# Group norm of the short convolution: products and copies four blocks ahead of the subtractions, and the gate norm's first sums of squares behind the gate's silu

## The chip, the cores and the metric

The kernel runs on one core of one Trainium2 chip. The metric is the device time of one execution in microseconds. The kernel before takes 1411.71 us (median of 3 runs, 1411.12 to 1412.81).

Engine names as the profile has them: PE is TensorE (matmuls; PEld is its weight load), DVE is VectorE, ACT is ScalarE, POOL is GpSimd, SP is the queue that issues most DMAs.

## The reference, cut to what matters

One layer over 1024 tokens of width 1024: a mixer, then a mixture of experts with 32 experts. The change touches the mixer, between its last projections and its output matmuls:

```python
def grouped_rmsnorm(x, g, n_groups):
    shp = x.shape
    xf = x.astype(jnp.float32).reshape(*shp[:-1], n_groups, shp[-1] // n_groups)
    y = xf * lax.rsqrt(jnp.mean(xf * xf, axis=-1, keepdims=True) + EPS)
    return (y.reshape(shp) * g.astype(jnp.float32)).astype(x.dtype)
...
    ssd_out = grouped_rmsnorm(y * jax.nn.silu(z), ssd_norm, SSD_GROUPS)
    sc = sc_b * causal_depthwise_conv(sc_c * sc_v, sc_conv_w)
    sc_out = grouped_rmsnorm(sc, sc_norm, SC_GROUPS)
    return jnp.concatenate([ssd_out, sc_out], axis=-1) @ w_out
```

`SSD_GROUPS` is 2 (groups of 512 columns), `SC_GROUPS` is 16 (groups of 64).

## The kernel before, in words

The tokens are worked through in two halves of 512 (`h` = 0 and 1). Each half runs 61 blocks of matmuls on PE, in a fixed order: 1 block `dt`, 12 `xbc`, 24 of the short convolution (`c`, `v`, `b`), 8 `z` (the gate), then `s` 0 to 3, `d` 0 to 3, `s` 4 to 7, `d` 4 to 7. The `s` and `d` blocks together are the output matmul: an `s` block multiplies the normed short convolution (`SCT`), a `d` block the normed gated part (`SST`), and both sum in one PSUM bank. The experts follow after the second half.

Everything is float32, split in two float32r parts: a matmul of two such numbers is three matmuls (high by high, high by low, low by high), so a block is 8 x 3 = 24 matmuls. The split of a 128x1024 piece of weights (`split_w`) is a copy on ACT (L80, `copy_a`) into the high half of a buffer `W` (four of them, `W[b % 4]`), and a subtraction on DVE (L86, `tt`) into the low half. In block n's turn the weights of block n + 3 are split.

The order of the work of each engine is the order in which the program issues it; each engine works in that order and waits by semaphores. The loop over blocks (`for n in range(NB)`) does in each turn: what follows from the block before (`post`), the block's matmuls, the load and split of weights ahead, and then the steps which a table has put on that turn (`at(n, f, ...)`, `todo`). The change is in that table. Steps around it, with b0 = 1 for the first half and 62 for the second, so that b0 + 41 is the sixth of the eight `z` blocks, b0 + 44 is the block `s` 0:

- `z_post` (L561): when the last of four `z` blocks is done, ACT takes the silu of its four PSUM banks into four temporaries, and DVE multiplies the four into `Y`. The last four silus stand in the turn of `s` 0, behind the weight copy of the turn before.
- `sc_norm_out` (lines 465 to 476): for each of 8 blocks j, DVE multiplies the short convolution by its weight and by its group's reciprocal root (L83, `SC<-SC,pc,P`), ACT copies the product into the high half of `SCT` (L80, `TB<-SC` in the first half, `TA<-SC` in the second), and DVE subtracts for the low half (L86). It is called for pairs of blocks: two products, two copies, two subtractions.
- `y_stats` (L568): sums of squares of `Y` on ACT, four for each group of 512 columns; the first group's need only the first four `z` blocks.
- `y_norm`: a square root on ACT (a table load, L90), a reciprocal on DVE (L91), and eight scalings of `Y` on DVE (L576), the first group's four ahead of the second's.
- `y_out` (L255): transposes of the scaled `Y` on PE, for columns 0 and 1 behind `s` 1, for 2 to 4 behind `s` 2, for 5 to 7 behind `s` 3.

PSUM has four banks `acc`. The four `z` banks are open until the last `z` block; the bank of `s` 0 is the first of these, free when the first silu has read it.

Of the kernel before, what the change touches and what calls it, by code (L numbers as in the profile page):

```python
# [36 lines left out]
def layer(ctx: ExitStack, tc: tile.TileContext, x, norm_mix, w_mix, ssd_conv_w, ssd_conv_b, dt_bias,  # L37
# [15 lines left out]
    def region(tag, shape, dt=F32):  # L53
        return rg.tile(shape, dt, name=tag, tag=tag)
# [24 lines left out]
    def copy_a(o, i, scale=1.0):  # L79
        act.activation(o, i, AF.Copy, scale=scale)  # L80

    def stt(o, a, s, b, op0, op1):
        dve.scalar_tensor_tensor(o, a, s, b, op0=op0, op1=op1)  # L83

    def tt(o, a, b, op):
        dve.tensor_tensor(o, a, b, op=op)  # L86
# [16 lines left out]
    def PC(i):  # L103
        return pc[:, i:i + 1]
# [143 lines left out]
    def halves(o, k, pt, scale):  # L248
        copy_a(o[:, 0, k], pt, scale=scale)
        stt(o[:, 1, k], pt, scale, o[:, 0, k].bitcast(F32), OP.mult, OP.subtract)  # L250
# [12 lines left out]
    def at(n, f, *a):  # L263
        todo.setdefault(n, []).append((f, a))
# [203 lines left out]
    def sc_norm_out(h, js):  # L468
        if js[0] == 0:
            SCT[h] = region(TA_IN[1 - h], [P, 2, KD, TB], FR)  # L470
        for j in js:
            o = SC[h][:, j]
            stt(o, o, PC(100 + j), RB[h][:, j], OP.mult, OP.mult)
            copy_a(SCT[h][:, 0, j], o)
        for j in js:
            tt(SCT[h][:, 1, j], SC[h][:, j], SCT[h][:, 0, j].bitcast(F32), OP.subtract)

# [409 lines left out]
    for h in range(2):  # L887
        b0 = h * HB + 1
        at(b0 + 1, dt_turn, h)
        at(b0 + 3, cum_mm, h)  # L890
        at(b0 + 4, cum_out, h)
        at(b0 + 37, sc_root, h)
        for u in range(8):
            at(b0 + max(11, 10 + 3 * u), ssd_seg_load, h, u)
            at(b0 + (12 + 3 * u if u else 13), ssd_decay, h, u)
            at(b0 + 13 + 3 * u, ssd_t, h, u)
            at(b0 + 14 + 3 * u, ssd_e, h, u)
            at(b0 + 15 + 3 * u, ssd_m, h, u)
            at(b0 + 16 + 3 * u, ssd_post, h, u)
        at(b0 + 38, silu_ready)  # L900
        for j in range(0, 8, 2):
            at(b0 + 41 + j // 4, sc_norm_out, h, (j, j + 1))
        at(b0 + 42, y_stats, h, 0)
        at(b0 + 44, y_stats, h, 1)
        at(b0 + 44, y_norm, h)
        for n, ks in ((45, (0, 1)), (46, (2, 3, 4)), (47, (5, 6, 7))):
            at(b0 + n, y_out, h, ks)
        at(b0 + 43, o_room, h)
        for j in range(8):
            nd = b0 + 48 + j + (4 if j > 3 else 0)  # L910
            at(nd - 1, x_load, h, j)
        if h == 1:
            for q, n in enumerate((44, 44, 45, 46, 51, 47, 49, 55, 56, 57, 57, 58, 58)):
                at(b0 + n, load_m, q)
            at(b0 + 50, h_diag)
        if h == 0:
            at(b0 + 46, lambda: X.__setitem__(1, region("SC", [P, KD, TB])))
            for q in range(4):
                at(b0 + 46, load_xT, 1, q)
            for i in range(NT):  # L920
                at(b0 + 5 + i, prep_stats, 1, i)
            at(b0 + 9, prep_root, 1, 0, 4)
            at(b0 + 45, g2_load)
            at(b0 + 51, root_first)
            for k in range(KD):
                at(b0 + 53 + k // 4, x_root, k)
            at(b0 + 56, lambda: XT.__setitem__(1, region(TA_IN[1], [P, 2, KD, TB], FR)))
            for k in range(KD):
                at(b0 + 56 + k // 2, lambda k=k: halves(XT[1], k, X[1][:, k], PC(k)))
            at(b0 + 28, route_load)  # L930
            at(b0 + 32, route_const)
            at(b0 + 46, route_weights)
            e0 = b0 + HB + 2
            at(e0 + 1, h_root, 0)
            at(e0 + 2, h_rows, 0)
            at(e0 + 3, h_cols, 0)
            at(e0 + 4, route_choose, 0)
            at(e0 + 6, route_pos_mm, 0)
            at(e0 + 7, route_gates, 0)
            at(e0 + 7, route_pos, 0)  # L940
            for part in range(2):
                at(e0 + 10 + part, route_tab, 0, part)
                at(e0 + 10 + part, route_tab_out, 0, part)
# [4 lines left out]
    for n in range(NB):  # L948
        kind, h, j = blocks[n][:3]
# [417 lines left out]
```

## Time and profile before

| what | us |
|---|---|
| median of 3 runs (lowest to highest) | 1411.71 (1411.12 to 1412.81) |
| the profiled execution's own time | 1409.6 |
| its span, from the first to the last instruction | 1407.8 |
| PE busy in the span | 1355.8 |
| DVE busy | 1047.1 |
| ACT busy | 888.2 |
| mean granted TensorE clock, share of full speed | 0.982 |

The span is what the trace shows; 1.8 us lie around it. A busy share is an average over stages; here what counts are the places where PE, the busiest engine, stands still. In a timeline each row is one instruction, or several alike in a row: start, length, engine, line, operation, tiles, and in brackets how long the engine was idle before it and what released it.

### The profile page before, as it was taken

Reading aid. Unit: us, or ns where it says so; the run is one execution under the profiler, and the core shown is the slowest. Engines: PE = TensorE matmul, PEld = TensorE weight load, DVE = VectorE, ACT = ScalarE, POOL = GpSimd, SP = SyncE. Lnnn points to the kernel's source line nnn. Section 1 sums busy time; section 2 is a strip of 40 time slices with the busy share of each in tenths; the row PEclk is TensorE's granted clock in tenths of the full one; section 3 lists DMA queues with packets and bytes.
Section 4 is the critical chain, followed back from the end, with each engine's and each line's share of the span. In section 5 each row is a group of like instructions: output and inputs, shape, how many; then the busy total and the mean of one; then the engine's idle time right before and its main releaser. Section 6 shows DMA issues by size and latency. Waiting matters only on the chain. (4 is left out here: it accounts for less than half of the span.)

```text
span 1407.8 us, 17291 instructions
## 1 busy us (share of the span) xinstructions
PE 1355.8 (96%) x6354; PEld 1071.5 (76%) x6354; DVE 1047.1 (74%) x1390; ACT 888.2 (63%) x1322; POOL 135.9 (10%) x124
## 2 busy tenths in 40 slices
PE   7999999989999999999999799999999999999992
PEld 5888887878878878788788677777777777777771
DVE  5776667574567776665643589999999999999985
ACT  6665443353475644344643488888888888888884
POOL 0000101000000000000000102211212211111110
PEclk9999999999999999999999899999999999999996
DMA  7243322534353232324556789999999999997996
GB/s 303 91 148 136 95 83 82 150 135 151 113 157 136 90 120 84 111 90 117 213 193 228 253 305 367 359 380 345 356 366 369 361 359 377 390 374 278 375 365 254
DMA packets 73176, 325.93 MB, mean 232 GB/s; under 512 B 11079, under 2 KB 27863, under 8 KB 40576
## 3 DMA queue, kind: packets, MB, share of 16 engines
q1 hardware_dynamic: 60816, 294.89, 55.9%
q0 software_dynamic: 12272, 29.90, 8.1%
q8 instruction: 51, 0.84, 0.2%
q14 instruction: 37, 0.30, 0.1%
HBM read 312.31 MB, written 29.49 MB: 243 GB/s over the span
## 5 line engine op out<-in xcount | busy, mean ns | idle before, releaser
L86 DVE TENSOR_TENSOR W<-WR,W 128x1024 fp32r<-128x1024 f32 x160 | 194.5, 1221 | 90.8 <-ACT W L80 90.3
L80 ACT ACTIVATE W<-WR 128x1024 fp32r<-128x1024 f32 x160 | 167.8, 1053 | 70.6 <-PE acc L270 37.0
L1182 PE MATMUL acc<-W,TB 128*112 128x512 f32 x512 | 204.7, 400 | 0.0
L1184 PE MATMUL acc<-W,TB 128*112 128x512 f32 x512 | 202.8, 396 | 0.0
L1183 PE MATMUL acc<-W,TB 128*112 128x512 f32 x512 | 200.8, 392 | 0.1
L269 PE MATMUL acc<-TB,W 128*128 128x512 f32 x416 | 166.7, 401 | 4.7 <-ACT tk L561 4.7
L269 PE MATMUL acc<-TA,W 128*128 128x512 f32 x416 | 166.1, 399 | 2.1 <-ACT tk L561 2.1
L271 PE MATMUL acc<-TA,W 128*128 128x512 f32 x416 | 162.9, 392 | 0.5 <-DVE W L86 0.5
L271 PE MATMUL acc<-TB,W 128*128 128x512 f32 x416 | 163.0, 392 | 0.0
L270 PE MATMUL acc<-TB,W 128*128 128x512 f32 x416 | 162.9, 392 | 0.0
L270 PE MATMUL acc<-TA,W 128*128 128x512 f32 x416 | 162.7, 391 | 0.0
L86 DVE TENSOR_TENSOR W<-SC,W 128x1024 fp32r<-128x1024 f32 x96 | 114.3, 1219 | 14.7 <-ACT W L80 14.7
L86 DVE TENSOR_TENSOR W<-Y,W 128x1024 fp32r<-128x1024 f32 x92 | 109.5, 1218 | 10.7 <-ACT W L80 10.5
L1183 PEld LDWEIGHTS acc<-W,TB 128*112 128x112 f32 x512 | 90.0, 176 | 28.7 <-DVE W L86 0.5
L1184 PEld LDWEIGHTS acc<-W,TB 128*112 128x112 f32 x512 | 89.2, 174 | 29.6 <-DVE TB L86 0.2
L1182 PEld LDWEIGHTS acc<-W,TB 128*112 128x112 f32 x512 | 89.2, 174 | 27.1 <-ACT TB L80 0.2
L86 DVE TENSOR_TENSOR W<-P,W 128x1024 fp32r<-128x1024 f32 (+1 forms) x82 | 96.0, 1196 | 13.0 <-ACT W L80 13.0
L1193 PE MATMUL sd<-W,TB 128*112 128x512 f32 x256 | 103.9, 406 | 0.8 <-ACT TB L80 0.6
L80 ACT ACTIVATE W<-SC 128x1024 fp32r<-128x1024 f32 x96 | 98.2, 1059 | 6.7 <-PE sd L1195 2.9
L1195 PE MATMUL sd<-W,TB 128*112 128x512 f32 x256 | 101.9, 398 | 0.0
L1194 PE MATMUL sd<-W,TB 128*112 128x512 f32 x256 | 101.2, 395 | 0.0
L80 ACT ACTIVATE W<-Y 128x1024 fp32r<-128x1024 f32 x92 | 94.8, 1060 | 10.0 <-PE sd L1195 4.0
(322 smaller groups left out, 2463.0 us busy)
## 6 DMA issues: line engine op xcount, KB each, us to landing
WR<-in_w_mix_dram SPq DMA_DIRECT2D x60, 1024.0 KB, 4.9
SC<-in_w_down_dram SPq DMA_DIRECT2D x18, 1024.0 KB, 7.5
SC<-in_w_gate_dram SPq DMA_DIRECT2D x16, 1024.0 KB, 7.6
P<-in_w_up_dram SPq DMA_DIRECT2D x16, 1024.0 KB, 7.4
Y<-in_w_up_dram SPq DMA_DIRECT2D x16, 1024.0 KB, 7.7
Y<-in_w_gate_dram SPq DMA_DIRECT2D x15, 1024.0 KB, 7.5
TA<-in_w_down_dram SPq DMA_DIRECT2D x15, 1024.0 KB, 8.0
Y<-in_w_down_dram SPq DMA_DIRECT2D x15, 1024.0 KB, 7.3
```

The source lines that it names most:

```text
L80: act.activation(o, i, AF.Copy, scale=scale)
L86: dve.tensor_tensor(o, a, b, op=op)
L269: pe.matmul(o, w[:, 0, k], t[:, 0, k], start=start and k == 0, stop=False)
L270: pe.matmul(o, w[:, 0, k], t[:, 1, k], start=False, stop=False)
L271: pe.matmul(o, w[:, 1, k], t[:, 0, k], start=False, stop=stop and k == KD - 1)
L1182: pe.matmul(pt, a[:, 0, k], w[:, 0, q], start=k == 0, stop=False)
L1183: pe.matmul(pt, a[:, 0, k], w[:, 1, q], start=False, stop=False)
L1184: pe.matmul(pt, a[:, 1, k], w[:, 0, q], start=False, stop=k == KD - 1)
L1193: pe.matmul(pt, a[:, 0, k], w[:, 0, n], start=k == 0, stop=False)
L1194: pe.matmul(pt, a[:, 0, k], w[:, 1, n], start=False, stop=False)
L1195: pe.matmul(pt, a[:, 1, k], w[:, 0, n], start=False, stop=k == 3)
```

## The change

The subtractions get a function of their own, `sc_norm_rest`, and the table is changed. Before: two pairs of blocks each in turns b0 + 41 and b0 + 42, and `y_stats` of the first group at b0 + 42. Now products and copies of blocks 0 to 3 stand in turn b0 + 41 with the subtractions of 0 and 1; the rest in b0 + 42; and the first group's `y_stats` is moved to b0 + 44, straight ahead of the second's.

```diff
@@ -472,6 +472,8 @@
             o = SC[h][:, j]
             stt(o, o, PC(100 + j), RB[h][:, j], OP.mult, OP.mult)
             copy_a(SCT[h][:, 0, j], o)
+
+    def sc_norm_rest(h, js):
         for j in js:
             tt(SCT[h][:, 1, j], SC[h][:, j], SCT[h][:, 0, j].bitcast(F32), OP.subtract)
 
@@ -898,9 +900,13 @@
             at(b0 + 15 + 3 * u, ssd_m, h, u)
             at(b0 + 16 + 3 * u, ssd_post, h, u)
         at(b0 + 38, silu_ready)
-        for j in range(0, 8, 2):
-            at(b0 + 41 + j // 4, sc_norm_out, h, (j, j + 1))
-        at(b0 + 42, y_stats, h, 0)
+        at(b0 + 41, sc_norm_out, h, (0, 1, 2, 3))
+        at(b0 + 41, sc_norm_rest, h, (0, 1))
+        at(b0 + 42, sc_norm_out, h, (4, 5))
+        at(b0 + 42, sc_norm_rest, h, (2, 3))
+        at(b0 + 42, sc_norm_out, h, (6, 7))
+        at(b0 + 42, sc_norm_rest, h, (4, 5, 6, 7))
+        at(b0 + 44, y_stats, h, 0)
         at(b0 + 44, y_stats, h, 1)
         at(b0 + 44, y_norm, h)
```

The order of the instructions changes on ACT and DVE alone, at one place in each half; on PE, POOL and SP every row stands where it stood. The two places of the first half follow (the second half's read alike, with `TA` for `TB`). Lines from 475 on are two higher in the changed kernel, so L563 is the silu that was L561 and L570 the sum of squares that was L568.

ACT, first half, from the weight copy of turn b0 + 41 to the square root of the gate norm; `TB<-SC` is the copy of a product into `SCT`, `W_84` the buffer of the weights of `s` 2, `tk<-acc` the silu. Before:

```order
L80 ACTIVATE W_82<-WR 128x1024
L80 ACTIVATE TB<-SC 128x512 x4
L80 ACTIVATE W_83<-WR 128x1024
L80 ACTIVATE TB<-SC 128x512 x4
L568 ACTIVATE junk,ssz<-Y 128x512 x4
L80 ACTIVATE W_84<-WR 128x1024
L561 ACTIVATE tk<-acc,rsx 128x512 x4
L80 ACTIVATE W_81<-WR 128x1024
L568 ACTIVATE junk,ssz<-Y 128x512 x4
L90 ACT_TABLE_LOAD
L90 ACTIVATE rsz<-ssz,eps 128x8
```

and of the change:

```order
L80 ACTIVATE W_82<-WR 128x1024
L80 ACTIVATE TB<-SC 128x512 x4
L80 ACTIVATE W_83<-WR 128x1024
L80 ACTIVATE TB<-SC 128x512 x4
L80 ACTIVATE W_84<-WR 128x1024
L563 ACTIVATE tk<-acc,rsx 128x512 x4
L80 ACTIVATE W_81<-WR 128x1024
L570 ACTIVATE junk,ssz<-Y 128x512 x8
L90 ACT_TABLE_LOAD
L90 ACTIVATE rsz<-ssz,eps 128x8
```

The four sums of the first group no longer stand ahead of the silu; all eight stand between the weight copy behind it and the square root.

DVE, first half, the same stretch, from the subtraction for the weights of `s` 0 to the multiplication of the silus into `Y`; `SC<-SC,pc,P` is a product, `TB<-SC,TB` a subtraction of the short convolution. Before:

```order
L86 TENSOR_TENSOR W_82<-WR,W_82 128x1024
L83 SCALAR_TENSOR_TENSOR SC<-SC,pc,P_1904 128x512 x2
L86 TENSOR_TENSOR TB<-SC,TB 128x512 x2
L83 SCALAR_TENSOR_TENSOR SC<-SC,pc,P_1904 128x512 x2
L86 TENSOR_TENSOR TB<-SC,TB 128x512 x2
L86 TENSOR_TENSOR W_83<-WR,W_83 128x1024
L83 SCALAR_TENSOR_TENSOR SC<-SC,pc,P_1904 128x512 x2
L86 TENSOR_TENSOR TB<-SC,TB 128x512 x2
L83 SCALAR_TENSOR_TENSOR SC<-SC,pc,P_1904 128x512 x2
L86 TENSOR_TENSOR TB<-SC,TB 128x512 x2
L86 TENSOR_TENSOR W_84<-WR,W_84 128x1024
L86 TENSOR_TENSOR Y<-Y,tk 128x512 x4
```

and of the change:

```order
L86 TENSOR_TENSOR W_82<-WR,W_82 128x1024
L83 SCALAR_TENSOR_TENSOR SC<-SC,pc,P_1904 128x512 x4
L86 TENSOR_TENSOR TB<-SC,TB 128x512 x2
L86 TENSOR_TENSOR W_83<-WR,W_83 128x1024
L83 SCALAR_TENSOR_TENSOR SC<-SC,pc,P_1904 128x512 x2
L86 TENSOR_TENSOR TB<-SC,TB 128x512 x2
L83 SCALAR_TENSOR_TENSOR SC<-SC,pc,P_1904 128x512 x2
L86 TENSOR_TENSOR TB<-SC,TB 128x512 x4
L86 TENSOR_TENSOR W_84<-WR,W_84 128x1024
L86 TENSOR_TENSOR Y<-Y,tk 128x512 x4
```

Two subtractions have moved from ahead of the weights of `s` 1 (`W_83`) to behind them, and the last products stand ahead of four subtractions instead of two.

## Rows read from the trace of the kernel before

**Rows 1.** Page: busy us of each engine, share of the span, instructions
```profile
PE 1355.8 (96%) x6354; PEld 1071.5 (76%) x6354; DVE 1047.1 (74%) x1390; ACT 888.2 (63%) x1322; POOL 135.9 (10%) x124
```

**Rows 2.** Waits of PE: line, releaser, us in total, times, longest us
```profile
PE acc L269 <- ACT tk L561: 6.8, 2, 4.7
```

**Rows 3.** Timeline of PE, first half, around the block s 0 and the first transposes
```profile
292.91 0.39 PE L290 MATMUL acc<-W,TA 128*128 128x512 f32 x1
...
293.59 0.39 PE L290 MATMUL acc<-W,TA 128*128 128x512 f32 x1
298.71 0.79 PE L269 MATMUL acc<-TB,W 128*128 128x512 f32 x1 [4.73 <-ACT tk L561]
...
312.04 1.03 PE L255 MATMUL sd<-ident,Y 128*128 128x128 f32 x8
312.83 0.48 PE L269 MATMUL acc<-TB,W 128*128 128x512 f32 x1
```

**Rows 4.** Timeline of PE, second half, the same places
```profile
685.99 0.39 PE L290 MATMUL acc<-W,TB 128*128 128x512 f32 x1
688.45 0.50 PE L269 MATMUL acc<-TA,W 128*128 128x512 f32 x1 [2.07 <-ACT tk L561]
...
701.87 0.48 PE L269 MATMUL acc<-TA,W 128*128 128x512 f32 x1
```

**Rows 5.** Timeline of ACT, first half, from the last copies to the square root's table
```profile
292.97 1.29 ACT L80 ACTIVATE TB<-SC 128x512 fp32r<-128x512 f32 x2 [1.42 <-DVE SC L83]
294.17 0.61 ACT L568 ACTIVATE junk<-Y 128x512 bf16<-128x512 f32 x1
...
297.04 1.04 ACT L80 ACTIVATE W<-WR 128x1024 fp32r<-128x1024 f32 x1
297.99 2.41 ACT L561 ACTIVATE tk<-acc,rsx 128x512 f32<-128x512 f32 x4
300.27 1.07 ACT L80 ACTIVATE W<-WR 128x1024 fp32r<-128x1024 f32 x1
301.21 0.64 ACT L568 ACTIVATE junk<-Y 128x512 bf16<-128x512 f32 x1
...
304.23 1.28 ACT L90 ACT_TABLE_LOAD   x1
```

**Rows 6.** Timeline of DVE, first half, the norm of the short convolution and the scalings
```profile
282.56 1.41 DVE L83 SCALAR_TENSOR_TENSOR SC<-SC,pc,P 128x512 f32<-128x512 f32 x2
284.00 1.35 DVE L86 TENSOR_TENSOR TB<-SC,TB 128x512 fp32r<-128x512 f32 x2
285.27 1.41 DVE L83 SCALAR_TENSOR_TENSOR SC<-SC,pc,P 128x512 f32<-128x512 f32 x2
...
288.33 1.23 DVE L86 TENSOR_TENSOR W<-WR,W 128x1024 fp32r<-128x1024 f32 x1 [0.26 <-ACT W L80]
...
306.09 3.25 DVE L576 TENSOR_SCALAR Y<-Y,rsz 128x512 f32<-128x512 f32 x8
```

**Rows 7.** Timeline of ACT, second half, the square root's table
```profile
693.70 1.28 ACT L90 ACT_TABLE_LOAD   x1
```

**Rows 8.** Timeline of DVE, second half, the first products and the scalings
```profile
672.38 1.41 DVE L83 SCALAR_TENSOR_TENSOR SC<-SC,pc,P 128x512 f32<-128x512 f32 x2
...
695.56 3.26 DVE L576 TENSOR_SCALAR Y<-Y,rsz 128x512 f32<-128x512 f32 x8
```

**Rows 9.** Stretches: us, PE, PEld, DVE, ACT, POOL busy (count); then PEclk, DMA share, GB/s
```profile
24.00:28.00 4.00, 3.28 (x19) 2.60 (x19) 2.37 (x10) 1.73 (x3) 0.00 (x0) 1.00 0.89 302
...
298.00:303.50 5.50, 4.79 (x11) 3.80 (x12) 4.77 (x6) 5.41 (x13) 0.00 (x0) 0.50 0.00 0
...
688.40:693.00 4.60, 4.55 (x13) 3.61 (x14) 4.32 (x6) 4.50 (x11) 0.00 (x0) 0.63 0.66 274
```

**Rows 10.** Timeline of PE, an early short pause
```profile
24.90 1.33 PE L234 MATMUL sd<-tk,ones 128*128 128x128 f32 x8 [0.72 <-DVE tk L233]
```

**Rows 11.** Waits of the SP queue: the loads of the experts' weights (L871)
```profile
SPq L871 <- DVE W L86: 452.8, 159, 14.5
```

## The prediction

> **What bounds the kernel now.** I read the page first: PE is busy for 96% of the span [rows 1], so time can come only from its pauses, from a lower clock behind them, or from its work, which the change leaves alone. The waits of PE come second: its largest wait in total is that of the first matmul of `s` 0 (L269) for the gate's silu on ACT (L561), twice, 6.8 us, the longest 4.7 [rows 2]. So the change sits at PE's costliest wait. Third, the timelines around them.
>
> At full clock matmuls follow each other every 0.227 us (three steps from 292.91 to 293.59 [rows 3]). In the first half the last matmul of `z` starts at 293.59; the next could start at 293.82 and starts at 298.71 [rows 3]: 4.89 us lost. In the second half it could start at 686.22 and starts at 688.45 [rows 4]: 2.23 us lost. A second loss follows the pause. The granted clock from 298 to 303.5 is 0.50, which is the 1.2 GHz level, and 0.63 in the mean from 688.4 to 693 [rows 9]. From the start of `s` 0 to that of `s` 2 there are 48 matmuls (48 x 0.227 = 10.88 us) and eight transposes (312.04 to 312.83, 0.79 us), 11.67 us at full clock. They take 312.83 - 298.71 = 14.12 [rows 3] and 701.87 - 688.45 = 13.42 [rows 4]: the clock costs 2.45 and 1.75.
>
> What holds the silu? ACT ends its last copy of the short convolution at 294.26, then does four sums of squares (294.17 to 297.04) and the weight copy for `s` 2 (297.04), and only then the silu, at 297.99; the matmul follows 0.72 later [rows 3, 5]. PE was done with `z` at 293.98. So four sums that nobody needs yet stand ahead of the silu, and behind the copies, which wait for products on DVE.
>
> **The change, part by part.** No instruction is added or taken away.
>
> *Sums moved.* Without them ACT goes from the last copy to the weight copy 2.87 us earlier (297.04 - 294.17) [rows 5].
>
> *Products and copies ahead.* On DVE two products take 1.44 us to the next row's start (282.56 to 284.00), two subtractions 1.27, a weight subtraction 1.23 in all [rows 6]. New order from 282.56: four products end at 285.44, two subtractions at 286.71. Copy 3 ends on ACT at 286.1 (the fourth product's end 285.4 and half of a pair's 1.29 [rows 5]), the weight copy for `s` 1 at 287.1 (1.04 [rows 5]); DVE waits 0.4 for it, instead of 0.26 now, and subtracts until 288.3. Two products, two subtractions, two products end at 292.45, and the last copy, 0.65 long, ends at 293.1 instead of 294.26. The weight copy then starts at about 293.05, since these two overlap a little now too (294.17 against 294.26 [rows 5]). The four subtractions at the end take DVE to 295.0, as before; the last is needed by the 23rd matmul of `s` 0, 5 us into the block.
>
> *Start of `s` 0, first half.* Weight copy at 293.05, silu at 294.0 (0.95 later, as now), matmul at 294.72 instead of 298.71: **3.99 us earlier**, 0.9 behind an unbroken run. A pause of 0.72 early in the kernel left the clock at 1.00 [rows 9, 10], and pauses of over 2 us brought it down [rows 3, 4, 9]. 0.9 is nearer to the first, so I take full clock: `s` 1 ends at 294.72 + 10.88 = 305.6.
>
> *What is late next.* The transposes behind `s` 1 need the scaled `Y`, and that chain now holds all eight sums. Silu at 294.0, weight copy 2.28 later, sums 0.94 after that at 297.22 [rows 5]. Four sums take 3.02 (301.21 to 304.23), eight 6.04: the square root's table at 303.26, 0.97 earlier than now. The scalings start as much earlier, at 305.12 instead of 306.09; four of eight in 3.25 us [rows 6] end at 306.75. The first transposes need only these four. Three can run ahead, and the fourth starts at about 306.8, so PE pauses some 1.2 us, and `s` 2 starts about 307.3 instead of 312.83: **5.5 us**. The cover for this chain was 312.04 - 306.09 - 1.6 = 4.3 us before; it is used up. Bounds for this half: a pause-free run would give 293.82 + 11.67 = 305.49, so 7.3; a clock as low as after the old pauses behind the first new one gives 307.35 to 308.05 for the end of `s` 1 and 308.1 to 308.8 for `s` 2, so 4.0 to 4.7.
>
> *Second half.* DVE's products start 672.38 - 282.56 = 389.82 later [rows 6, 8], so a free silu would start at 683.8, while PE ends `z` only at 686.38 [rows 4]. The first bank of `z` is done 18 matmuls before the last, so its silu is over in time and `s` 0 starts unbroken at 686.22; `s` 1 ends at 697.1. The fourth silu waits for the last matmul and ends near 687.1; weight copy, sums from 687.95, eight until 693.99, 0.29 later than now [rows 7]. The scalings start at 695.85 [rows 8], four end at 697.5, and `s` 2 starts at about 698.0 instead of 701.87: **3.85 us**. Bounds: 698.0 moves to 697.89 without the wait, and to 699.9 if all eight scalings were needed.
>
> *Queues.* No DMA moves in the order. The WR loads wait for weight subtractions, and these come earlier by 1 to 4 us. A sum's scratch tile comes from a pool of four which the silus use too: the first sum now waits for the first multiplication into `Y`, which ends about 296.8, 0.4 ahead of its turn; that costs nothing, and if that margin is gone, tenths.
>
> *Sum.* 5.5 + 3.85 = **9.35 us** from an execution of 1409.6, whose span is 1407.8. All later work follows PE, so I carry the gain to the end. The median is 2.1 us above that execution, so 1411.71 - 9.35 = **1402.4**. A measurement of this kernel can tell about 0.2% from no change, 2.8 us.
>
> **The rivals.**
>
> *B: the short pauses cost clock too.* First half alone, where pauses of 0.9 and 1.2 us stand: 1.75 to 2.45 more than forecast, **1404.1 to 1404.8**, if it falls behind the second (behind the first, the wait of the transposes covers 1.2 of it). For it: 1.2 lies between the 0.72 that cost nothing [rows 9, 10] and the 2.07 that cost 1.75 [rows 4]. The Trainium skill, "TensorE: Matmul & The Clock Gate", section "A second HAM failure mode: psum-queue depth-cycling", speaks against this change: brief pauses between groups of matmuls that go round the PSUM banks make the clock swing between its levels, and the time is lost between the bursts. By that rule B or E below is the case; with the 0.72 pause the trace does not agree, and for 0.9 and 1.2 it is silent.
>
> *C: the gate norm takes more back.* If the transposes need all eight scalings, `s` 2 starts at 308.4 + 0.8 = 309.2 and 699.1 + 0.8 = 699.9: gains of 3.6 and 2.0, **1406.1**. For it: both waits sit on that chain. Against: each scaling writes a row block and column group of its own, and the first transposes read those of group 0 alone.
>
> *D: the experts' weights bind.* Their first loads go into the buffers freed by the last subtractions of the second half's norm, which come earlier by the first half's 5.5 us alone; were that stream the bound, the second half's gain would go: 1411.71 - 5.5 = **1406.2**. Against: 159 of these loads wait for a buffer that DVE frees, 452.8 us in all [rows 11], so the stream follows the engines.
>
> *E, the other side: the clock stays low.* Two pauses in place of one, 13 us apart, hold PE at 1.2 GHz through `s` 0 and `s` 1 of both halves. A matmul there takes 0.43 instead of 0.227, 0.2 more. 48 of them end at 294.72 + 20.5 and 686.22 + 20.5, with the transposes `s` 2 starts at 316.0 and 707.5: 3.2 and 5.6 later than now, **1420.5**. It decides from about 68 slowed matmuls: 61 for the 9.35 and 2.8 us, and 7 which the wait for the transposes covers. Against: after the longest pause the low clock lasted to about 303.5, some 11 matmuls [rows 9].
>
> *F: the change does not do what it says:* the silu gives PE nothing, because another wait behind it ends as late as 298.7. No row shows one; **1411.7**.
>
> **How the numbers follow.** Forecast 0.60, B 0.19, C 0.06, D 0.05, F 0.05, E 0.05. The first four are faster by over 0.2%: 0.90; F is within 0.2%: 0.05; E slower: 0.05. The range runs from the pause-free bounds (7.3 + 4.0 = 11.3 us, 1400.4) to C and D with the runs' spread of 0.8: 1400.4 to 1407.0; F and E lie outside.
>
> **What would show it.** Right: on ACT the weight copy of `s` 2 straight behind the last copy and the silu near 294.0; PE's wait for L561 at about 0.7 to 0.9 in the first half and gone in the second; a new wait of PE's transposes (L255) for DVE's scaling of `Y`, about 1 us and tenths; clock at 1.00 behind the pauses; eight sums in one row of 6 us; `s` 2 near 307.3 and 692.5 (698.0 less the first half's gain). Wrong: the clock at half behind `s` 0 (B, E), the transposes behind the eighth scaling (C), gaps of PE or ACT on DMAs among the experts (D), or `s` 0 released by anything other than the silu (F).

## The result and the profile after

The changed kernel takes **1402.86 us** (median of 4 runs, 1401.02 to 1404.48) against 1411.55 for the kernel before beside it (4 runs, 1411.12 to 1412.81): a ratio of 0.9934 [0.9922, 0.9945]. The forecast was 1402.4 us. The profiled execution, the fastest of the four, took 1401.02 us with a span of 1399.2, 8.6 less than before; the mean granted clock rose from 0.982 to 0.986.

Busy us, share and instructions by engine, on the page of after, to be read beside [rows 1]:

```profile
PE 1353.4 (97%) x6354; PEld 1068.7 (76%) x6354; DVE 1045.4 (75%) x1390; ACT 887.7 (63%) x1322; POOL 136.6 (10%) x124
```

No engine has other work than before. Two waits answer to [rows 2]; line, releaser, us in total, times, longest:

```profile
PE acc L269 <- ACT tk L563: 0.4, 1, 0.4
...
PEld sd L255 <- DVE Y L578: 0.7, 3, 0.3
```

PE's wait for the gate's silu has gone from 6.8 us in two places to 0.4 in one, and a new wait of 0.7 us stands at the transposes, for the scaling of `Y`. The timeline of PE in after, at the places of [rows 3] and then of [rows 4]:

```profile
293.90 0.39 PE L290 MATMUL acc<-W,TA 128*128 128x512 f32 x1
294.69 0.50 PE L269 MATMUL acc<-TB,W 128*128 128x512 f32 x1 [0.40 <-ACT tk L563]
...
305.71 1.74 PE L255 MATMUL sd<-ident,Y 128*128 128x128 f32 x8
307.20 0.48 PE L269 MATMUL acc<-TB,W 128*128 128x512 f32 x1
...
680.37 0.39 PE L290 MATMUL acc<-W,TB 128*128 128x512 f32 x1
680.59 0.39 PE L269 MATMUL acc<-TA,W 128*128 128x512 f32 x1
...
691.48 1.05 PE L255 MATMUL sd<-ident,Y 128*128 128x128 f32 x8
692.29 0.48 PE L269 MATMUL acc<-TA,W 128*128 128x512 f32 x1
```

First half: `s` 0 starts 0.79 after the last matmul of `z`, one step of 0.23 and 0.56 lost, where it was 5.12. Its 48 matmuls then take 305.71 - 294.69 = 11.02, and the transposes 1.49 to the start of `s` 2, where they took 0.79. Second half: `s` 0 follows `z` one step later, nothing is lost, and the transposes take 0.81. `s` 2 starts 5.63 earlier than before in the first half (307.20 for 312.83) and 9.58 earlier in the second (692.29 for 701.87).

The timeline of ACT in after, at the place of [rows 5], and the square root's table of the second half, the place of [rows 7]:

```profile
291.82 1.30 ACT L80 ACTIVATE TB<-SC 128x512 fp32r<-128x512 f32 x2 [1.23 <-DVE SC L83]
293.02 1.05 ACT L80 ACTIVATE W<-WR 128x1024 fp32r<-128x1024 f32 x1
293.97 2.40 ACT L563 ACTIVATE tk<-acc,rsx 128x512 f32<-128x512 f32 x4
...
297.20 0.64 ACT L570 ACTIVATE junk<-Y 128x512 bf16<-128x512 f32 x1
...
303.09 1.28 ACT L90 ACT_TABLE_LOAD   x1
...
688.17 1.28 ACT L90 ACT_TABLE_LOAD   x1
```

The weight copy stands straight behind the last copy, the silu straight behind it, and the eight sums in one row from 297.20 to 303.09. DVE in after, at the place of [rows 6], with the products, subtractions and scalings that the steps speak of:

```profile
282.98 2.73 DVE L83 SCALAR_TENSOR_TENSOR SC<-SC,pc,P 128x512 f32<-128x512 f32 x4
...
292.36 2.49 DVE L86 TENSOR_TENSOR TB<-SC,TB 128x512 fp32r<-128x512 f32 x4
...
304.95 3.26 DVE L578 TENSOR_SCALAR Y<-Y,rsz 128x512 f32<-128x512 f32 x8
```

The stretches of after behind the two old pauses (us, then PE, PEld, DVE, ACT, POOL busy with counts, PEclk, DMA share, GB/s), to be read beside [rows 9]:

```profile
294.00:298.00 4.00, 3.60 (x17) 2.74 (x16) 4.00 (x7) 3.97 (x9) 0.00 (x0) 1.00 0.00 0
298.00:303.50 5.50, 5.50 (x26) 4.57 (x25) 1.53 (x2) 5.32 (x15) 0.00 (x0) 1.00 0.56 183
303.50:312.00 8.50, 8.36 (x40) 6.57 (x39) 7.05 (x13) 4.34 (x6) 0.00 (x0) 1.00 0.84 315
686.00:693.00 7.00, 7.00 (x36) 5.86 (x35) 3.17 (x9) 5.49 (x11) 0.00 (x0) 1.00 0.97 407
```

The clock is full in all of them; before it was 0.50 and 0.63.

From `s` 2 of the second half to the end the two traces differ by 9.58 - 8.6 = 0.98 us the other way: after loses that much among the experts. Between the transposes of the 21st and of the 31st expert it loses more, 179.42 us against 178.07 in before; 0.4 are lost ahead of that stretch, and 0.7 come back behind it. Whether the change causes that was the open question, and the last experiments are about it.

### The profile page after: what moved, and what is told of

Its sections match the earlier page's. It is cut to its first block, busy times and chain, and to the rows that moved or that the text cites. A ratio compares the mean times of both kernels' runs of the same rounds, so it can differ in the third digit from the quotient of the medians.

```text
span 1399.2 us, 17295 instructions
## 1 busy us (share of the span) xinstructions
PE 1353.4 (97%) x6354; PEld 1068.7 (76%) x6354; DVE 1045.4 (75%) x1390; ACT 887.7 (63%) x1322; POOL 136.6 (10%) x124
```

## The experiments

Three landmarks run through them. Y0 and Y1 are the starts of the first transposes of `Y` (L255) in the first and the second half, 312.04 and 701.08 in before, 305.71 and 691.48 in after. The third is the time T from the 21st expert's first transposes to the 31st's. Further traces of before put Y1 at 700.93 and 701.47, so a gain at Y1 carries a few tenths of uncertainty. Some of that is there from the start of the kernel: an early row of PE (L528, in the changed kernel L530) stands at 105.09 in before, at 105.32 to 105.41 in three more traces of the old order, at 105.35 in after and at 105.97 in e3. Medians of one kernel differ by more than 1 us. Ratios are against the kernel before on the same chip.

### The two parts alone

**e1_sums**, the sums moved and nothing else, from the kernel before:

```diff
-        at(b0 + 42, y_stats, h, 0)
+        at(b0 + 44, y_stats, h, 0)
```

> Only the sums of squares are moved behind the silu; products, copies and subtractions stay in pairs. Theory (the sums and the copies are two separate holds of the silu): in the first half the silu starts near 295.1 and s 0 near 295.9 instead of 298.7, a pause of about 1.9 us that brings the clock to half for 8 to 12 matmuls as the pause of 2.07 did; s 2 starts near 309.3 to 310.0 (after: 307.2). In the second half s 0 runs on without a pause, as after, since PE itself ends z later than ACT is free. Gain at the second half's s 2 6.8 to 8.4 us (after: 9.6), in the median 5.5 to 8 us. Rival (the copies are the hold that counts, the sums only fill ACT's wait for DVE): s 0 stays near 298 in the first half, and the gain is under 3 us.

**e2_copies**, the products and copies ahead and the sums where they were, from the changed kernel:

```diff
-        at(b0 + 44, y_stats, h, 0)
+        at(b0 + 42, y_stats, h, 0)
```

> Only products and copies are put ahead; the first group's sums stay in front of the silu. Theory: the last copy ends 1.2 us earlier, the silu and s 0 come 1.1 us earlier in both halves, the pauses stay at about 3.6 and 1.0 us, the clock still falls to half in the first half (2 us lost) and perhaps stays full in the second. Transposes wait for nothing. Gain at the second half's s 2 2.2 to 3.9 us, in the median about as much. Rival (the copies are the hold that counts): gain over 6 us.

Measured: e1 1405.74 us, ratio 0.9948 [0.9935, 0.9962]; e2 1408.38, 0.9975 [0.9965, 0.9985]. PE's timeline and two stretches of e1:

```profile
296.26 0.80 PE L269 MATMUL acc<-TB,W 128*128 128x512 f32 x1 [2.17 <-ACT tk L561]
...
308.77 1.03 PE L255 MATMUL sd<-ident,Y 128*128 128x128 f32 x8
309.56 0.48 PE L269 MATMUL acc<-TB,W 128*128 128x512 f32 x1
...
693.84 1.12 PE L255 MATMUL sd<-ident,Y 128*128 128x128 f32 x8
```

```profile
294.00:298.00 4.00, 1.83 (x5) 1.45 (x5) 3.71 (x6) 3.97 (x8) 0.00 (x0) 0.76 0.03 10
298.00:303.50 5.50, 5.50 (x22) 4.43 (x22) 2.43 (x4) 5.34 (x14) 0.00 (x0) 0.87 0.37 115
```

and the same of e2:

```profile
297.22 0.80 PE L269 MATMUL acc<-TB,W 128*128 128x512 f32 x1 [2.97 <-ACT tk L563]
...
309.56 1.03 PE L255 MATMUL sd<-ident,Y 128*128 128x128 f32 x8
...
684.41 0.50 PE L269 MATMUL acc<-TA,W 128*128 128x512 f32 x1 [0.51 <-ACT tk L563]
...
695.44 1.03 PE L255 MATMUL sd<-ident,Y 128*128 128x128 f32 x8
```

```profile
298.00:303.50 5.50, 5.50 (x22) 4.44 (x21) 3.40 (x5) 5.39 (x12) 0.00 (x0) 0.81 0.16 39
684.00:692.00 8.00, 7.59 (x33) 6.30 (x34) 5.36 (x9) 7.88 (x16) 0.00 (x0) 1.00 0.84 326
```

In the first half each part shortens the pause (PE idle for 2.17 and 2.97 us instead of 4.73), and behind both rests the clock still falls. At the start of `s` 0 the parts add up: 2.45 us earlier (e1) and 1.49 (e2), and the change 4.02. At Y0 they gain 3.27 and 2.48, together 5.75; the change has 6.33 there, since its clock stays full, and 5.63 at `s` 2, since its new wait takes 0.70 back. In the second half e1 gains 701.08 - 693.84 - 3.27 = 3.97, as much as the whole change (9.58 - 5.63 = 3.95), and e2 gains 701.08 - 695.44 - 2.48 = 3.16. In these traces the parts do the same work twice there: either one takes the silu out of PE's way or nearly so, and the rest of 0.51 in e2 leaves the clock at 1.00.

That overlap is not seen in the medians: e1 and e2 gain 6.25 and 3.61 us (from 1411.99), together 9.86, and the change gains 8.69 and, in after_again below, 9.40. e2's trace is of the fastest of its eleven executions (1405.42; the slowest took 1411.18), and where the others lost more is not on record.

e1 came as expected. e2's trace did not: it has 5.64 us at `s` 2 of the second half (696.23 for 701.87), and 2.2 to 3.9 were expected; its median lies within that range. The upper end had the full clock of the second half in it. Mis-sized was the rest: `s` 0 came some 1.5 us earlier in each half instead of 1.1, and the low clock of the first half cost 1.46 instead of 2. Behind the pause of 0.51 the clock does not fall, and 1.60 of the 1.75 us that it cost in this half come back with the pause.

### The new wait at the transposes

**e3_early** takes the change and puts the first group's sums ahead of everything, in the turn b0 + 40, where ACT has nothing to do:

```diff
-        at(b0 + 44, y_stats, h, 0)
+        at(b0 + 40, y_stats, h, 0)
```

> The changed kernel with the first group's sums two turns earlier than they were before the change, in the turn b0 + 40, where ACT stands idle for 6.4 us (first half) and 3.9 us (second half) ahead of the weight copy for s 0. Theory (what the change leaves is a wait of the transposes for the gate norm, because all eight sums stand in its chain): the root comes 3 us earlier than after, the wait of the transposes, 0.7 us in the first half, is gone, and s 2 starts near 306.5 instead of 307.2; the second half, where the transposes run on, is as after. Gain over the changed kernel 0.5 to 0.8 us at the second half's s 2. Rival (these transposes are held by something else than the norm): no gain. If the loads of the experts' weights bind in the last experts, the end gives back most of it: the median is then the changed kernel's within 0.5 us.

Measured: 1402.38 us, 0.9931 [0.9918, 0.9945]. PE of e3, first half:

```profile
295.73 0.50 PE L269 MATMUL acc<-TB,W 128*128 128x512 f32 x1 [0.87 <-ACT tk L563]
...
306.75 1.03 PE L255 MATMUL sd<-ident,Y 128*128 128x128 f32 x8
307.54 0.48 PE L269 MATMUL acc<-TB,W 128*128 128x512 f32 x1
```

The stretch of e3 from `s` 0 on, behind the pause of 0.87 us, has the full clock:

```profile
295.70:299.00 3.30, 3.27 (x14) 2.74 (x15) 3.30 (x6) 3.27 (x7) 0.00 (x0) 1.00 0.00 0
```

ACT, behind the issue of the load that it waits for (SPq is the queue of SP):

```profile
266.89 0.33 SPq L147 DMA_DIRECT2D WR<-in_w_mix_dram  x1
281.79 1.06 ACT L80 ACTIVATE W<-WR 128x1024 fp32r<-128x1024 f32 x1 [4.14 <-DMA WR<-in_w_mix_dram]
...
301.25 1.28 ACT L90 ACT_TABLE_LOAD   x1
```

The table comes 1.84 us earlier than in after (301.25 for 303.09), and the transposes take 0.79 again: the wait of 0.70 is gone. Yet `s` 2 starts at 307.54, later than after's 307.20, because `s` 0 starts 1.04 later. The rows of ACT say why. Everything here starts with ACT's copy of the weights of `s` 0, which waits for their load, and ACT could begin it 1.04 later than in after:

```profile
266.27 0.33 SPq L147 DMA_DIRECT2D WR<-in_w_mix_dram  x1
280.75 1.06 ACT L80 ACTIVATE W<-WR 128x1024 fp32r<-128x1024 f32 x1 [6.54 <-DMA WR<-in_w_mix_dram]
```

From this copy to `s` 0 it is 13.94 us in both kernels, and to `s` 2 25.75 in e3 against 26.45 in after: 0.70 gained, and all of it covered by the lateness of this one execution. Of the 1.04, 0.62 were there when the load was issued, and as much already at PE's row at 105 us (105.97 for 105.35); the rest is the load's own. So the 0.5 to 0.8 us expected at `s` 2 of the second half do not show there, where e3 is 0.35 later than after. The medians cannot tell the two kernels apart. The silu's first waiting point is thus a DMA, which the prediction had not named.

### The norm ahead of that load

**e8_ahead** puts the whole norm of the short convolution and the first sums one turn earlier, so that ACT and DVE do them while that load is still under way:

```diff
-        at(b0 + 41, sc_norm_out, h, (0, 1, 2, 3))
-        at(b0 + 41, sc_norm_rest, h, (0, 1))
-        at(b0 + 42, sc_norm_out, h, (4, 5))
-        at(b0 + 42, sc_norm_rest, h, (2, 3))
-        at(b0 + 42, sc_norm_out, h, (6, 7))
-        at(b0 + 42, sc_norm_rest, h, (4, 5, 6, 7))
-        at(b0 + 44, y_stats, h, 0)
+        at(b0 + 40, y_stats, h, 0)
+        at(b0 + 40, sc_norm_out, h, (0, 1, 2, 3))
+        at(b0 + 40, sc_norm_rest, h, (0, 1))
+        at(b0 + 41, sc_norm_out, h, (4, 5))
+        at(b0 + 41, sc_norm_rest, h, (2, 3))
+        at(b0 + 41, sc_norm_out, h, (6, 7))
+        at(b0 + 41, sc_norm_rest, h, (4, 5, 6, 7))
```

> The changed kernel with the whole norm of the short convolution and the first group's sums one turn earlier: the sums, products 0 to 3 with their copies and subtractions 0 and 1 in turn b0 + 40, the rest in b0 + 41. DVE stands idle there for 6.3 us (first half) and 3.8 us (second half) behind the weights of the last z block, while in the changed kernel the products wait behind the weights of s 0, whose load lands only at 280.3 us. Theory (what is left of the first pause comes from that load, what is left of the second from the eight sums in the norm's chain): the last copy ends before 290, s 0 follows z without a pause, the transposes without a wait, s 2 starts near 305.5 instead of 307.2, the second half's near its pause-free bound; PE's gain at the second half's transposes 10.9 to 11.3 us (changed kernel: 9.6). The last experts then give back more, 2 to 3 us, since the weight loads start no earlier than the norm lets them: median 0.5 to 1.5 us below the changed kernel's. Rival (the products wait for the broadcast of the roots, which lands as late as the weights): nothing gained in the first half.

Measured: 1402.22 us, 0.9922 [0.9909, 0.9936]. PE and DVE of e8, first half:

```profile
294.02 0.39 PE L290 MATMUL acc<-W,TA 128*128 128x512 f32 x1
294.25 0.39 PE L269 MATMUL acc<-TB,W 128*128 128x512 f32 x1
...
305.13 1.03 PE L255 MATMUL sd<-ident,Y 128*128 128x128 f32 x8
305.92 0.48 PE L269 MATMUL acc<-TB,W 128*128 128x512 f32 x1
```

```profile
279.42 2.74 DVE L83 SCALAR_TENSOR_TENSOR SC<-SC,pc,P 128x512 f32<-128x512 f32 x4 [3.83 <-DMA P<-rb_d]
```

`s` 0 follows `z` without a pause in the first half too, and no wait is left at the transposes. Y1 is at 690.24, 10.84 earlier than in before and 1.24 earlier than in after. The waits that the change left were therefore worth some 1.2 us of PE's path. DVE's first products now wait for the load of the reciprocal roots (`rb_d`), and PE no longer waits for what follows from them. By the medians e8 is 0.9 us faster than the changed kernel on the same chip (1402.22, and 1403.13 in after_again below), and the intervals overlap. The span of its trace is nevertheless 1401.0, longer than after's, because 2.9 us are lost behind the 31st expert (44.24 us to the last hidden transposes, 41.36 in after). That led back to the experts.

### Where the experts lose it

My theory was rival D in a small form: the change brings PE forward against a stream of weights that cannot follow. The other reading was that the loss falls on either kernel by chance. The place it could come from is the look-ahead of the loads, which falls from eight half-weights to four at half number 150 of 192 (`Q1`); behind it the DMA pauses. One stretch of before shows it (columns as in [rows 9]):

```profile
1260.00:1280.00 20.00, 20.00 (x95) 15.29 (x94) 18.34 (x20) 16.95 (x20) 3.35 (x2) 1.00 0.62 201
```

DMA is busy for 0.62 there, and for 1.00 or thereabouts in the next three such stretches. **e4_after_q170** lets the look-ahead fall later in the changed kernel, **e5_before_q170** in the kernel before, by the same line, and **after_again** is the changed kernel once more:

```diff
-    LEAD, FALL, Q1, LEAD1, TAGS = 8, 16, 150, 4, ("TA", "WR", "P2", "P1")
+    LEAD, FALL, Q1, LEAD1, TAGS = 8, 16, 170, 4, ("TA", "WR", "P2", "P1")
```

> The changed kernel, with the point from which the experts' weight loads look only 4 halves ahead (Q1) put from the 150th to the 170th half; nothing else. Theory (the 1.4 us that the changed kernel loses between 1315 and 1340 us are waits for weights: the loads pause for some 8 us around 1265, when the look-ahead shrinks, and the DMA engines, busy all the time before and after, don't catch up): the pause of the loads moves to about 1320, the waits of ACT for weight loads in the last experts shrink from some 9 us to under 3, PE's gain of 9.2 us stays until at least 1340, and the median is 1.0 to 1.5 us below the changed kernel's. Rival (the 1.4 us are chance of one execution, or contention with the gathers): median as the changed kernel's within 0.5 us, and the same waits for weights.

> The changed kernel once more, as the measure for the three others on the same chip. Theory: s 2 near 307.2 and the second half's transposes near 691.5 again, clock at 1.00 behind both short pauses, and PE's gain of 9.2 to 9.6 us shrinks by 1 to 2 us among the last five experts, where ACT waits for weight loads. Rival (the loss among the last experts was chance): the gain at the last expert's transposes is 9 us or more.

> Control: the kernel before, with the look-ahead of the weight loads shrinking at the 170th half instead of the 150th. Theory (the stream binds only because PE comes earlier): the kernel before lost nothing there, its last experts follow each other every 17.8 us, so the change of Q1 is worth under 0.5 us here. Rival (the late shrinking is simply better, whatever PE does): it gains 1 us or more here too.

**e9_ahead_q170** has e8's table and this line.

> Both: the norm one turn earlier, and Q1 at 170. Theory: PE's gain of about 11 us is kept until the last experts, the median is 10.5 to 11.5 us below the kernel before and 1.5 to 2.5 below the changed kernel. Rival (the weight stream as a whole binds, not the pause in it at 1265): the median stays within 0.7 us of the changed kernel's with Q1 at 170 alone, some 10.2 us below the kernel before.

**before_look1**, **before_look2** and **after_look3** are single executions of the unchanged kernels, for their traces.

> The kernel before, one more execution. Theory (the change brings PE ahead of the experts' weight loads): from the transposes of the 21st expert to those of the 31st it takes 178.1 us as in the first trace, within 0.2. Rival (the loss among the last experts comes by chance to either kernel): over 178.5 here or in the next.

> The kernel before, a third execution; expectations as for the one before it: 178.1 us within 0.2 by the theory, over 178.5 in one of the two by the rival.

> The changed kernel, a third execution. The first two took 179.4 and 178.2 us from the 21st to the 31st expert's transposes. Theory: again over 178.1, by 0.1 to 1.5 us. First half: s 2 near 307.2, clock full behind both short pauses.

**e10_ahead_q180** has e8's table and `Q1` at 180.

> The best kernel so far (norm one turn earlier, Q1 at 170) with Q1 at 180. Theory (the loads' pause only has to come late): 178.1 us between the 21st and the 31st expert, median within 1 us of the kernel with 170, or above it, as the pause now falls together with the loads of the final norm. Rival (each later shrinking is worth something): 1 us or more below it.

Measured, with T and the span from the trace of each (one execution, so T is one sample):

| kernel | Q1 | Y1 | T | span | median | ratio |
|---|---|---|---|---|---|---|
| before | 150 | 701.08 | 178.07 | 1407.8 | | |
| before_look1 | 150 | 700.93 | 179.14 | 1410.5 | 1412.32, one run | |
| before_look2 | 150 | 701.47 | 178.96 | 1409.7 | 1411.51, one run | |
| after | 150 | 691.48 | 179.42 | 1399.2 | 1402.86 | 0.9934 [0.9922, 0.9945] |
| after_again | 150 | 691.52 | 178.19 | 1399.2 | 1403.13 | 0.9934 [0.9920, 0.9948] |
| after_look3 | 150 | 691.81 | 178.89 | 1402.0 | 1403.78, one run | |
| e8_ahead | 150 | 690.24 | 178.54 | 1401.0 | 1402.22 | 0.9922 [0.9909, 0.9936] |
| e5_before_q170 | 170 | 701.47 | 178.06 | 1410.2 | 1411.30 | 0.9988 [0.9979, 0.9998] |
| e4_after_q170 | 170 | 691.61 | 178.07 | 1399.8 | 1401.61 | 0.9928 [0.9915, 0.9942] |
| e9_ahead_q170 | 170 | 689.97 | 178.06 | 1397.7 | 1399.70 | 0.9912 [0.9898, 0.9925] |
| e10_ahead_q180 | 180 | 690.58 | 178.07 | 1395.8 | 1397.41 | 0.9898 [0.9881, 0.9914] |

My theory fell. The kernel before loses about a microsecond at the same place in two traces of three; the trace that stands ahead of the prediction happened to be the one without it, and the changed kernel's second trace (after_again) is nearly without it too. What such a loss looks like in before_look1, by waits and by a row of PE in the middle of an expert:

```profile
ACT W L80 <- DMA Y<-in_w_up_dram: 4.3, 4, 1.7
```

```profile
1315.15 0.49 PE L1194 MATMUL sd<-W,TB 128*112 128x512 f32 x1 [0.46 <-DVE W L86]
```

and in after:

```profile
ACT W L80 <- DMA Y<-in_w_up_dram: 3.8, 3, 1.9
ACT W L80 <- DMA SC<-in_w_up_dram: 2.8, 2, 1.7
```

```profile
1322.94 0.49 PE L1200 MATMUL sd<-W,TB 128*112 128x512 f32 x1 [0.48 <-DVE W L86]
```

The same kind of weight, one expert later, the same wait of ACT, and PE held by a split that stands behind the copies of halves that landed late. In before this wait of ACT for `in_w_up` is 0.7 in all. T is 178.06 or 178.07 in every kernel with `Q1` at 170 or 180, in both orders of the norm, and anything from 178.07 to 179.45 (e2) with `Q1` at 150. e5, the control, gained 0.12% [0.02%, 0.21%], 1.2 us by the medians, where I had expected less than half a microsecond: the kernel before has the flaw as well. So it is a flaw of its own, and what the change gains is not given back there. e9 gained more than expected, 12.8 us on the kernel before (10.5 to 11.5) and 3.4 on after_again (1.5 to 2.5), though these two intervals just overlap.

T does not hold all of the loss. Behind the 31st expert PE waits once more, for ACT to read a bank (L1217, in the changed kernel L1223), which stands behind copies of late halves: 1.01 and 1.34 us in before_look1 and before_look2, 1.57 in after_look3, 1.65 in e3 (where ACT had waited 1.1 us for a half of `in_w_down`), 1.21 in e8, and with `Q1` at 170 still 0.88 in e4 and 0.46 in e9. Of the 3.3 us between the spans of e8 and e9, T has 0.48 and the stretch behind it 2.0.

The pause does not vanish; it moves. With `Q1` at 170 (e9) it stands 40 us later, with 180 (e10) later still and shallower (0.86 from 1320, 0.80 from 1340). From 1260, where before has 0.62, both have 1.01:

```profile
1300.00:1320.00 20.00, 20.00 (x96) 15.26 (x95) 18.01 (x18) 17.33 (x22) 4.59 (x3) 1.00 0.57 192
1320.00:1340.00 20.00, 20.00 (x95) 15.33 (x94) 18.34 (x19) 17.31 (x21) 1.78 (x2) 1.00 0.86 300
```

Of ACT's waits for the experts' weights, one of 0.3 us is left in e10, for a half of `in_w_down`.

**e10 is the fastest kernel here: 1397.41 us** (4 runs, 1396.83 to 1397.52) against 1411.44 for the kernel before beside it, 14.0 less, and its times lie closest together. Against e9 I had expected no more than 1 us; by the ratios it is about 2, but the two ran on different chips and the intervals overlap (0.9898 [0.9881, 0.9914] and 0.9912 [0.9898, 0.9925]). That the last ten halves of look-ahead are worth something is likelier by this than not, and not settled. e4 against after_again, 1401.61 and 1403.13, also overlaps.

## Why the prediction was right

It forecast 1402.4 us by a gain of 9.35; the trace has 9.58 at `s` 2 of the second half, and the medians differ by 8.69 (1411.55 - 1402.86). By its steps:

- *Sums moved, products and copies ahead.* Forecast: weight copy at 293.05, silu at 294.0, `s` 0 at 294.72. Trace: 293.02, 293.97, 294.69. This is closer than the working deserves. DVE's products began 0.42 later than in before (282.98 for 282.56), since the weights of `s` 0 came in later, and made it up: with the products ahead, a subtraction no longer waits for its own copy on ACT. Four take 2.49 us, against two in 1.35 [rows 6], and four products take 2.65 (282.98 to 285.63), where I had put twice 1.44, which holds such a wait.
- *Start of `s` 0.* The pause lost 0.56 instead of 0.9, because `z` ended 0.3 later than in the trace of before shown; four traces of the old order have its last matmul at 293.59 to 293.93, so as much comes without the change, most of it from the start of the kernel (105.35 for 105.09 at PE's early row). I took full clock behind it, by the nearest row, 0.72 [rows 10]; the granted clock is 1.00 in all four stretches. This step decided between the forecast and B or E.
- *What is late next.* Forecast: a new pause at the transposes, 1.2 us, by the scaling chain; three of them run in it, so that `s` 2 comes 0.9 late (307.3 for 305.6 + 0.79). Trace: 0.70 late, since eight sums took 5.89 instead of 6.04, the table came at 303.09 (forecast 303.26) and the scalings at 304.95 (305.12), and `s` 1 ended 0.1 later. `s` 2: 307.20, forecast 307.3. The gain of the first half is 5.63, forecast 5.5. That this wait is the scaling chain's, e3 shows: the sums earlier, and it is gone.
- *Second half.* Forecast: no pause, a wait of 0.11 at the transposes, 3.85. Trace: no pause, 0.02 at the transposes, 3.95. `s` 2 at 692.29, forecast 692.5.
- *Sum.* "All later work follows PE" held: between Y1 and the first expert before and after take 104.56 and 104.58 us. A loss like the 0.98 of the span behind it comes and goes in either kernel.

Two parts of the argument were thinner than they looked. I derived the median from one execution by its offset of 2.1 us, without knowing that the shown trace of before was a lucky one: three traces of before have a mean span of 1409.3, three of after 1400.1, 9.2 apart. And "a silu that waits for copies, which wait for products" stopped one step short of its origin: the products stand behind a weight copy that waits for a DMA. Here the copy came 0.43 later than in before (280.75 for 280.32), which the shorter steps made up; in e3 it came 1.04 later still, and `s` 0 with it.

The rivals: B, that short pauses cost clock, was hardly tried by the change itself, which had 0.40 us idle ahead of `s` 0 and three waits of at most 0.3 at the transposes, with the clock at 1.00. It fell with pauses of the size that it spoke of, behind which the clock is 1.00 too: 0.87 in e3 and 1.01 to 1.65 in the last experts (last section). The Trainium skill's "TensorE: Matmul & The Clock Gate", section "A second HAM failure mode: psum-queue depth-cycling", tells of a kernel whose brief pauses between groups of matmuls come often enough to make the clock swing. The traces do not show that for single pauses of up to 1.65 us, and no run here tries pauses that come often. C fell: the last of the first eight transposes had started by 307.20, and the eighth scaling ended at 304.95 + 3.26 = 308.21. D fell: 8.6 of the 9.58 us are left at the end of the trace, and by before_look1, before_look2 and e5 the loss among the experts is the kernel before's too. E needed a low clock and there was none. F fell with the first row of waits.

## What to carry to other kernels

When a stalled matmul waits for work on another engine, list what stands ahead of that work in the engine's queue and who needs it: here sums and subtractions that nobody needed yet cost PE 9.6 us, of which 4.0 as clock behind the pauses (2.31 and 1.72, in the two traces shown). Work the next deadline out before moving anything behind (the sums' cover was 4.3 us, of which all was used), and follow the chain back until it reaches a load or the start, not only to the first busy engine. And take a second and third trace of the kernel before ahead of any story about a microsecond: an effect that shows in one trace of each kernel may belong to neither.

## What the runs showed of the hardware that was not expected

The length of a pause counts. Behind idle times of 0.40, 0.51 and 0.87 us the granted clock stayed at 1.00; behind 2.07 [rows 4] and 2.17 (e1) it fell, at a cost of 1.75 and 1.6 us, nearly as much as the pause itself. The last experts have pauses of lengths between these, each in an unbroken run of matmuls: 1.01 us (before_look1), 1.21 (e8), 1.34 (before_look2), 1.57 (after_look3) and 1.65 (e3). The longest, a row of PE in e3 and the stretch behind it:

```profile
1348.93 0.49 PE L1199 MATMUL sd<-W,TB 128*112 128x512 f32 x1 [1.65 <-ACT g L1223]
```

```profile
1348.90:1354.90 6.00, 5.97 (x31) 4.72 (x32) 5.12 (x6) 5.65 (x8) 1.56 (x1) 1.00 1.03 337
```

The clock is 1.00 for some 6 us behind each of the five. At the last expert's hidden transposes (L1209, in the changed kernel L1215) two pauses follow each other within 1.3 us. Behind 1.68 and 0.63 (e10) and behind 1.82 and 0.63 (e2) the clock is 0.72 in the mean of 6 us, and behind 1.88 and 0.63 (e3) it is 1.00. So a single pause of up to 1.65 us cost no clock in these traces, every one from 2.07 to 5.24 us ahead of `s` 0 did (six traces), and between the two no one length divides.

Nor did the price grow much with the length: behind 4.73 to 5.24 us it was 1.76 to 2.45 in four traces of the old order (13.43 to 14.12 us from `s` 0 to `s` 2, for 11.67 at full clock). Bringing a pause down to where the clock holds pays twice: e2 took 1.6 us off the second half's and gained 1.60 of its 1.75 of clock. Shortening one that stays above pays less: e1 took 2.45 us off the first half's pause, and its clock still cost 1.63 there, 0.1 to 0.8 less than in those four traces.

The load of 1 MB of weights for `s` 0 let ACT begin its copy at 280.32 to 281.16 in four traces of the old order and at 280.75 to 281.79 in after and e3, a spread of more than a microsecond that everything behind it inherits where nothing else is ready. Part of it is there when the load is issued, between 266.00 and 266.89; the load itself takes 14.2 us in before, 14.4 in after and 14.8 in e3, and the median of its kind is 4.9 (before). It runs beside the broadcast of the reciprocal roots, for which DVE waits too once it is ready early (3.83 us in e8). That the two loads share bandwidth there is likely by this, and was not tried.
